# RWKV beta-alpha products made beside the operands, key norms at the key strips, and a 128-row rotary low product

## The chip, the cores and the metric

The kernel is one launch on one core of a Trainium2 chip. The metric is the device time of one execution in microseconds, the median of three runs. Everything is float32; large products are split into a high and a low part (fp32r), so that one product is three matmuls: high by high, low by high, high by low.

## The reference, cut to what matters

Two stacks of layers run one after the other: two hybrid layers, and then four layers of three kinds (SGU, RWKV-7, MLA, SGU) on 512 tokens and 256 context tokens, width 1024. The change touches the RWKV layer and the attention of the MLA layer.

```python
def rwkv7_features(h, mu, w_in, w_lora1, w_lora2, w0, a_lora1, a_lora2, a0, k_k, k_a):
    xx = center_shift(h)
    xs = h[:, :, None, :] + xx[:, :, None, :] * mu
    rkvz = jnp.einsum('blcd,cde->blce', xs[:, :, :4], w_in)
    ...
    decay = jnp.exp(-jnp.exp(log_w.astype(jnp.float32)))
    a = jax.nn.sigmoid(a0[:, None, None, :] + ...)
    kk = split_heads(k * k_k).astype(jnp.float32)
    kk = (kk * lax.rsqrt(jnp.sum(kk * kk, axis=-1, keepdims=True) + 1e-12)).reshape(k.shape)
    k_dir = k * (1 + (a - 1) * k_a)

    def step(S, inp):                       # rwkv7_scan, over time, 2 directions, 16 heads
        w_t, k_t, v_t, kk_t, a_t = inp[:5]
        s_kk = jnp.einsum('nbhvk,nbhk->nbhv', S, kk_t)
        S = S * w_t[..., None, :] - s_kk[..., :, None] * (kk_t * a_t)[..., None, :] + v_t[..., :, None] * k_t[..., None, :]
        y_t = jnp.einsum('nbhvk,nbhk->nbhv', S, inp[5]) if emit else None
        return S, y_t
```

In MLA each head's key has 128 plain and 64 rotary features (`k = concat(k_nope, k_rope)`), and the scores are a product over both.

## The kernel before, in words

The 768 tokens (512 and 256 of context, `T`) are cut into `NS` = 12 steps of `CH` = 64. The features are cut into `KD` = 8 blocks of 128, which are two heads each. The state's recurrence over a step of 64 tokens is turned into products of four operands per direction d: alpha (kk, scaled by decays up to the step) and r, kept side by side in `st_ar`, and beta (kk times a) and k, kept in `st_bk`. `operands(f)` makes them for block f and both directions and stores them to DRAM (`rw_ar`, `rw_bk`).

`features` runs the strips in the order k, r, z, v (8 each; a strip is 48 matmuls). Between the strips it takes turns of `lora`, `operands`, `by_tokens` (the values turned to token order, in the v strips) and `first`. The order of TensorE's instructions is that of the code (`in_order`); the turns are handed out by credits (`OPS`, `PACE`). `operands` has the lora products (L1563) with their tanh (L1564), the norm of the keys by `head_scale` (sums L1233, a reciprocal square root of 12 columns on VectorE L187 to L192, and its spreading over the features L1241, L1245), the decays' scan over time (L1586, L1588), three exponentials (L1594, L1596, L1598), the products (L1604 GpSimd, L1605, L1606, L1609 VectorE) in two parts of 512 and 256 columns, and the stores (L1610 to L1615). `st_ar` and `st_bk` have one buffer each.

`scan` runs 9 slots p. In each, `lanes` steps through block p's first six time steps and block p-1's last six, and side work is woven in: `ahead` (loads and products G, GR, TK for coming steps, L1692 to L1739), `output` of block p-2, and for block p+1 and p+2 the matrix that solves each step's inner recurrence. That is in three parts: `pairs` (L1764: beta times alpha of each step, 64 by 64, from operands read back from DRAM, masked and stored as 32 x 32 blocks to `rw_md`), `inverse` (reads `rw_md`, inverts the 32 x 32 triangles by 31 pairs of vector instructions, stores to `rw_mt`) and `merge` (puts the blocks together with two small products, L1822 and L1834). For block 0 all three and for block 1 the first two are done in the v strips by `first`. SyncE issues all these loads and stores in one queue, in order.

In the MLA heads `attend` computes 64 rows of scores, each over 512 and 256 keys, from five matmuls: three for the plain part, one for the rotary high part over 128 rows (`kr`), and one for the rotary low part over the 64 rows of the head (`krl`), L2284. `by_features` makes `kr` and `krl`; weights are split beside it (`weight_pool`, two raw buffers).

## Time and profile before

| what | value |
|---|---|
| median of 3 runs | 4303.05 us (4300.52 to 4309.85) |
| profiled execution | 4307.25 us, its span 4305.5 us |
| TensorE busy | 3947.2 us, 92% |
| VectorE, ScalarE, GpSimd busy | 2538.4, 1557.5, 1333.9 us |
| RWKV operands beside r and z strips | 2160 to 2450 us |
| v strips | 2452 to 2569 us |
| scan, slots 0 to 8 | 2569 to 3120 us |
| MLA heads | about 3310 to 3890 us |

The times of a trace count from the start of the span. PE is TensorE's matmuls, PEld its weight loads, DVE VectorE, ACT ScalarE, POOL GpSimd, SP SyncE, whose rows are DMA issues. A row of a table of stretches gives its bounds, its length, and then what each engine was busy, with the number of instructions; PEclk is the granted TensorE clock as a share of 2.4 GHz. A row of groups gives line, engine, operation, output and input with their tiles, the count, busy time, mean ns of one, and the idle time in front of them with what ended it. In a timeline row an idle time in front stands in brackets.

### The profile page before, as it was taken

The page shows a single profiled execution, that of the slowest core. Times are in us where ns is not written, and L with a number is a line of the kernel's source. Part 1 is how long each engine was busy: PE and PEld are TensorE (multiplying, and loading weights), DVE is VectorE, ACT ScalarE, POOL GpSimd, SP SyncE. Part 2 cuts the span into 40 slices and gives each one's busy share as a digit, 9 for nine tenths or more (in the row PEclk, how much of TensorE's full clock was granted, in tenths as well). Part 3 has the DMA queues.
Part 4 walks back from the last instruction along what each step waited for, and adds up shares of the span by engine and source line. Part 5 has one row for each costly group of instructions (what it writes and reads, how often), then busy time and mean ns, then how long its engine had stood idle before and what let it go on. Part 6 is the DMA issues. An engine that isn't in the chain of part 4 may idle for free.

```text
span 4305.5 us, 66606 instructions
## 1 busy us (share of the span) xinstructions
PE 3947.2 (92%) x25974; PEld 3217.2 (75%) x25974; DVE 2538.4 (59%) x5080; ACT 1557.5 (36%) x2952; POOL 1333.9 (31%) x1365
## 2 busy tenths in 40 slices
PE   8799999889999999998877787888789999998999
PEld 7777777776877788887755676667567788876887
DVE  7726445765554534445689734677654677784544
ACT  4244223334332322222455322343243455553222
POOL 3321111322211211113455545674122344442221
PEclk9899999899999999999988897999889999999999
DMA  3125543112365321122256676765224121221232
GB/s 90 43 76 159 170 136 90 50 60 94 102 197 157 107 64 59 59 63 86 68 170 182 201 199 152 178 163 123 74 57 127 36 60 49 60 75 52 88 93 88
DMA packets 615143, 447.41 MB, mean 104 GB/s; under 512 B 205469, under 2 KB 544173, under 8 KB 614829
## 3 DMA queue, kind: packets, MB, share of 16 engines
q1 hardware_dynamic: 612236, 438.95, 35.0%
q0 software_dynamic: 2592, 4.20, 0.5%
q8 instruction: 205, 3.36, 0.3%
q14 instruction: 110, 0.89, 0.1%
HBM read 371.76 MB, written 67.11 MB: 102 GB/s over the span
## 4 chain that ended last, share of the span: by engine, by line
PE 75%; DVE 12%; DMA 4%; issue 3%; ACT 3%; POOL 2%; SPq 1%; DVEq 0%; ACTq 0%; POOLq 0%
PE acc L160 54%; PE wide L2284 3%; PE wide L160 2%; PE acc L1717 2%; PE aux L1853 2%; PE po L2332 2%; DMA G<-rw_ar 1%; PE aux L920 1%; PE aux L2309 1%; DVE xs L1347 1%; DVE wlo L141 1%; PE aux L1064 1%; DVE st_bk L1606 1%; DMA rw_bk<-st_bk 1%; DMA ar<-rw_ar 1%
## 5 line engine op out<-in xcount | busy, mean ns | idle before, releaser
L138 ACT CAST whi<-wraw 128x1024 fp32r<-128x1024 f32 (+3 forms) x471 | 456.7, 970 | 1186.5 <-PE acc L160 956.8
L141 POOL TENSOR_TENSOR wlo<-wraw,whi 128x1024 fp32r<-128x1024 f32 (+2 forms) x205 | 427.3, 2085 | 1374.8 <-ACT whi L138 1232.2
L160 PE MATMUL acc<-hh,whi 128*128 128x512 f32 (+2 forms) x1776 | 628.9, 379 | 10.3 <-ACT hh L421 5.0
L160 PE MATMUL acc<-hl,whi 128*128 128x512 f32 (+2 forms) x1776 | 625.4, 377 | 2.5 <-DVE hl L422 2.5
L160 PE MATMUL acc<-hh,wlo 128*128 128x512 f32 (+2 forms) x1776 | 624.7, 376 | 1.7 <-DVE wlo L141 1.7
L141 DVE TENSOR_TENSOR wlo<-wraw,whi 128x1024 fp32r<-128x1024 f32 (+3 forms) x266 | 323.3, 1217 | 469.6 <-ACT whi L138 429.4
L160 PEld LDWEIGHTS acc<-hh,whi 128*128 128x128 f32 (+1 forms) x1776 | 317.2, 189 | 86.8 <-ACT whi L138 16.7
L160 PEld LDWEIGHTS acc<-hh,wlo 128*128 128x128 f32 (+1 forms) x1776 | 316.9, 189 | 64.8 <-DVE wlo L141 2.4
L160 PEld LDWEIGHTS acc<-hl,whi 128*128 128x128 f32 (+1 forms) x1776 | 316.7, 189 | 64.2 <-DVE hl L422 4.1
L160 PE MATMUL acc<-whi,hh 128*128 128x256 f32 (+1 forms) x896 | 295.7, 332 | 2.3 <-ACT hh L967 2.3
L160 PE MATMUL acc<-wlo,hh 128*128 128x256 f32 (+1 forms) x896 | 294.8, 329 | 0.0
L160 PE MATMUL acc<-whi,hl 128*128 128x256 f32 (+1 forms) x896 | 289.4, 326 | 0.4 <-DVE hl L968 0.4
L988 DVE SCALAR_TENSOR_TENSOR xT<-acc,mod,xT 128x512 f32<-128x512 f32 x256 | 185.6, 746 | 134.5 <-PE acc L160 133.7
L160 PEld LDWEIGHTS acc<-whi,hh 128*128 128x128 f32 x896 | 176.3, 197 | 20.3 <-ACT hh L967 4.6
L160 PEld LDWEIGHTS acc<-wlo,hh 128*128 128x128 f32 x896 | 176.6, 197 | 14.1 <-issue 0.7
L160 PEld LDWEIGHTS acc<-whi,hl 128*128 128x128 f32 x896 | 174.9, 196 | 14.6 <-DVE hl L968 1.1
L160 PE MATMUL wide<-xsl,whi 128*128 128x512 f32 (+1 forms) x512 | 141.5, 359 | 31.2 <-POOL xsl L1349 26.2
L160 PE MATMUL wide<-xsh,whi 128*128 128x512 f32 (+1 forms) x512 | 145.9, 368 | 20.4 <-ACT xsh L1348 15.8
L160 PE MATMUL wide<-xsh,wlo 128*128 128x512 f32 (+1 forms) x512 | 140.0, 356 | 3.1 <-POOL wlo L141 2.7
L160 PE MATMUL acc<-ffgh,whi 128*128 128x512 f32 x352 | 139.9, 400 | 0.0
L160 PE MATMUL acc<-ffgl,whi 128*128 128x512 f32 x352 | 138.4, 395 | 0.0
L160 PE MATMUL acc<-ffgh,wlo 128*128 128x512 f32 x352 | 138.3, 395 | 0.0
(627 smaller groups left out, 8972.0 us busy)
## 6 DMA issues: line engine op xcount, KB each, us to landing
ada_w<-in_ada_w SPq DMA_DIRECT2D x32, 1536.0 KB
wraw<-in_sgu_w_in SPq DMA_DIRECT2D x96, 512.0 KB
wraw<-in_w_up SPq DMA_DIRECT2D x88, 512.0 KB
wraw<-in_w_in SPq DMA_DIRECT2D x44, 512.0 KB
wraw<-in_w_down SPq DMA_DIRECT2D x32, 512.0 KB
wraw<-in_sgu_w_out SPq DMA_DIRECT2D x32, 512.0 KB
...
```

Source lines behind the costliest of these rows:

```text
L138: nc.scalar.copy(hi, raw)
L141: eng.tensor_tensor(lo, raw, hi.bitcast(F32), ALU.subtract)
L160: mm(out, lhsT=a, rhs=b[:, t0:t1], start=first and n == 0, stop=last and n == 2)
L920: nc.tensor.matmul(ps[32 * t:32 * t + 32, :384], lhsT=self.sc[:, k * 2 + j, :], rhs=raw[:, j, t * 384:t * 384 + 384], start=k + j == 0, st ...
L988: nc.vector.scalar_tensor_tensor(dst[k], ps, m[:, 16 + k, j:j + 1], dst[k], ALU.mult, ALU.add)
L1064: nc.tensor.matmul(ps[:, c * 128 - t0:c * 128 - t0 + 128], lhsT=v[c][:, ft * 128:ft * 128 + 128], rhs=wst[:, f2, :], start=True, stop=True)
L1347: nc.vector.scalar_tensor_tensor(t[:, t0:t0 + n], self.xx[k][:, t0:t0 + n], mu, src[k], ALU.mult, ALU.add)
L1606: nc.vector.scalar_tensor_tensor(o_(bk[:, s0:s1, 0]), i_(ta[d], t0, n), 0.5, i_(b, t0, n), ALU.mult, ALU.mult)
L1717: nc.tensor.matmul(pk[:, (s - s0) * 256:(s - s0) * 256 + 256], lhsT=bk[:, d, s].rearrange("p q x -> p (q x)"), rhs=G[:, :, d, s], start=Tr ...
L1853: mm = lambda o, d, e, a, b, first=False, last=True: nc.tensor.matmul((ps if o else py)[h[e], o * 128 + d * 64:o * 128 + d * 64 + 64], lhs ...
L2284: nc.tensor.matmul(sc[:, k0:k1], lhsT=a, rhs=b[:, k0:k1], start=j == 0, stop=j == 4)
L2332: nc.tensor.matmul(o, lhsT=a[:, b], rhs=x[:, b], start=b + j == 0, stop=b == NT2 - 1 and j == 2)
```

## The change

Five things are done. (1) The sums for the key norms are made at the k strips (`key_squares`, `key_sums`), and one reciprocal square root over all 96 columns follows at the first r strip; `operands` only spreads them. (2) In `operands` the scan over time runs in place; the exponentials go to a padded tile `eb`, of which a view shifted by one step replaces the subtraction and the third exponential; the products run over all 768 columns; the ec copy goes to GpSimd; the reordering of the chunks moves into the stores (eight in place of four for d = 0). (3) `pairs` and its loads are gone. `within` makes the same products from `st_ar` and `st_bk` in SBUF, called one or two turns after the operands of a direction are made, and stores the diagonal blocks to `md[f]` and the one other block that is needed to `mo[f]`; `merge` reads it from there. No mask is applied, since only the lower parts are read. (4) `inverse` of block p+2 is woven over the whole slot, not its second half, and `first` has one inverse and one merge and no pairs. (5) `krl` has 128 rows and two buffers, and the heads' weights one raw buffer.

```diff
+    def within(self, f, d, ar, bk, tmp):
+        net, nc = self.net, self.net.nc
+        M, hf = tmp(), (slice(0, 64), slice(64, 128))
+        for n0, n in ((0, 8), (8, 4)):
+            pg = net.aux()
+            for s in range(n0, n0 + n):
+                c = s if d else (s - 4) % NS
+                for e in range(2):
+                    nc.tensor.matmul(pg[hf[e], (s - n0) * CH:(s - n0) * CH + CH], lhsT=bk[hf[e], c, 0], rhs=ar[hf[e], c, 0], start=True, stop=True)
+            nc.scalar.copy(M[:, n0 * CH:(n0 + n) * CH], pg[:, :n * CH])
+        Mt = M.rearrange("p (s t) -> p s t", t=CH)
+        for e in range(2):
+            for h in range(2):
+                q = 64 * e + 32 * h
+                nc.sync.dma_start(self.blocks(self.md[f], e, h)[:, d * NS:d * NS + NS], Mt[q:q + 32, :, 32 * h:32 * h + 32])
+            nc.sync.dma_start(self.mo[f][e][:, d * NS:d * NS + NS], Mt[64 * e:64 * e + 32, :, 32:64])
...
+    def key_sums(self, f, sq):
+        nc, ps = self.net.nc, self.net.aux()
+        two = self.bones.rearrange("p (e c) -> p e c", c=64)[:, :, 0]
+        for c in range(NS // 2):
+            nc.tensor.matmul(ps[:, 2 * c:2 * c + 2], lhsT=sq[:, c * 128:c * 128 + 128], rhs=two, start=True, stop=True)
+        nc.vector.tensor_scalar(self.ky[:, f * NS:f * NS + NS], ps[:, :NS], 1.0, 1e-12, ALU.mult, ALU.add)
...
+                if (name, f) == ("r", 0):
+                    net.rsqrt(self.kr, self.ky, Renamed(self.ap, {"rsq_i": "vt", "rsq_t": "vb"}), KD * NS)
...
 # operands
-            return ap.tile([128, T], F32, tag="f", name="tmp", bufs=5)
+            return ap.tile([128, T], F32, tag="f", name="tmp", bufs=4)
...
-        sq = tmp()
-        nc.scalar.activation(sq, kt, AF.Square, scale=col(P["kk"], f))
-        yield
+        if f:
+            yield
+            self.pending()
+            yield
...
-            nc.gpsimd.tensor_tensor(ld, b, ld, ALU.subtract)
...
-            nc.vector.tensor_copy(self.ec[:, f, :, d], ar[:, :, 1, CH - 1])
...
-            nc.scalar.activation(ld, ld, AF.Exp)
...
-            for t0, n, s0, s1 in parts:
-                nc.gpsimd.tensor_tensor(o_(bk[:, s0:s1, 1]), i_(kd, t0, n), i_(b, t0, n), ALU.mult)
-                nc.vector.tensor_tensor(o_(ar[:, s0:s1, 1]), o_(ar[:, s0:s1, 1]), i_(rt, t0, n), ALU.mult)
-                nc.vector.scalar_tensor_tensor(o_(bk[:, s0:s1, 0]), i_(ta[d], t0, n), 0.5, i_(b, t0, n), ALU.mult, ALU.mult)
+            nc.gpsimd.tensor_tensor(o_(bk[:, :, 1]), ch(kd), ch(b), ALU.mult)
+            nc.vector.tensor_tensor(o_(ar[:, :, 1]), eb[:, :, 1:CH + 1], ch(rt), ALU.mult)
+            nc.vector.scalar_tensor_tensor(o_(bk[:, :, 0]), ch(ta[d]), 0.5, ch(b), ALU.mult, ALU.mult)
+            yield
+            nc.vector.tensor_tensor(o_(ar[:, :, 0]), eb[:, :, 2 * d:2 * d + CH], ch(kq), ALU.mult)
...
+            for c0, c1, s0 in parts:
+                at = slice(s0, s0 + c1 - c0)
+                nc.sync.dma_start(steps(self.d["ar"][d, rows, :])[:, at], ar[:, c0:c1])
+                nc.sync.dma_start(steps(self.d["bk"][d, r0:r0 + 64, :])[:, at], bk[0:64, c0:c1])
+                for q in range(2):
+                    nc.sync.dma_start(steps(self.d["bk"][d, r0 + 64:r0 + 128, :])[:, at, 1 - q, :], bk[64:128, c0:c1, q, :])
+            self.pending = partial(self.within, f, d, ar, bk, tmp)
...
 # scan
-                    side += [(pairs(p + 2), 16, PW[0], PW[1]), (inverse(p + 2), 33, 0.5, 1.0)]
+                    side.append((inverse(p + 2), 33))
...
 # MLA
-            with net.weight_pool(2, 3, 3), net.psum(na, nb, nw), ...
+            with net.weight_pool(1, 3, 3), net.psum(na, nb, nw), ...
...
-                    ops = ((ah[:, ct], kh), (ah[:, ct], kl), (al[:, ct], kh), (qs[:, v, ct], kr), (qs[r, v, ct], self.krl[r]))
+                    ops = ((ah[:, ct], kh), (ah[:, ct], kl), (al[:, ct], kh), (qs[:, v, ct], kr), (qs[:, v, ct], krl))
...
-            nc.vector.tensor_tensor(lo[r, t0:t1], ps[r, :t1 - t0], hi[r, t0:t1].bitcast(F32), ALU.subtract)
+            nc.vector.tensor_tensor(lo[:, t0:t1], ps[:, :t1 - t0], hi[:, t0:t1].bitcast(F32), ALU.subtract)
```

On TensorE, in the r strips of the kernel before, one block of operands has these instructions (`hw` and `ha` are the lora products, `bones` the norm's sums, `hs_rep` its spreading; L160 are the strips):

```order
L160 MATMUL wide<-xsh,wlo 128x256
L1563 MATMUL aux<-hw,w_17460 128x512 x2
L1563 MATMUL aux<-hw,w_17460 128x256 x2
L1233 MATMUL aux<-bones,tmp 128x2 x6
L1563 MATMUL aux<-ha,a_17461 128x512 x2
L1563 MATMUL aux<-ha,a_17461 128x256 x2
L160 MATMUL wide<-xsh,whi 128x512
...
L1245 MATMUL aux<-ident,hs_rep 128x128 x6
```

None of them reads a product of the block before. In the changed kernel the same place on TensorE reads as follows (L1668 are the 24 matmuls of one direction, from `st_ar` and `st_bk`):

```order
L160 MATMUL wide<-xsh,wlo 128x256
L1668 MATMUL aux<-st_ar,st_bk 64x64 x24
L1592 MATMUL aux<-hw,w_17559 128x512 x2
L1592 MATMUL aux<-hw,w_17559 128x256 x2
L160 MATMUL wide<-xsh,whi 128x512
...
L1592 MATMUL aux<-ha,a_17560 128x512 x2
L1592 MATMUL aux<-ha,a_17560 128x256 x2
L1253 MATMUL aux<-ident,hs_rep 128x128 x6
L160 MATMUL wide<-xsh,whi 128x512
...
L1668 MATMUL aux<-st_ar,st_bk 64x64 x24
```

The first set is the second direction of the block before, and the lora products of the next block stand directly behind it; the last row is the first direction of that block, three quarters of a strip later.

On SyncE, in slot 1 of the scan, the queue of the kernel before has the store of an inverse (`rw_mt`) ahead of the loads of G (`ar` and `bk` are the loads of `pairs`):

```order
L1676 DMA bk_22141<-rw_bk 128x512
L1798 DMA rw_mt<-invT 96x1024
L1677 DMA ar_22142<-rw_ar 128x4x64
L1797 DMA rw_mt<-invA 96x1024
L1702 DMA G_20707<-rw_ar 64x2x512 x2
L1739 DMA SV<-rw_vt 64x4x64 x4
L1739 DMA VU<-rw_vt 64x4x64 x4
L1774 DMA rw_md<-xx_21242 32x24x32 x4
```

This is the inverse of block 2. In the changed kernel the inverse of block 2 is stored in the v strips already, and that of block 3 in slot 0, where SyncE has this:

```order
L1746 DMA G_20318<-rw_ar 64x2x512 x2
L1783 DMA SV<-rw_vt 64x4x64 x4
L1783 DMA VU<-rw_vt 64x4x64 x4
L1811 DMA rw_mt<-invT 96x1024
L1810 DMA rw_mt<-invA 96x1024
L1823 DMA xx_21694<-rw_mo_16222 32x768
L1736 DMA bk_21609<-rw_bk 128x2x512
```

The pairs' loads and the stores of `rw_md` are gone from the scan, and the inverses stand about one block earlier in the queue.

## Rows read from the trace of the kernel before

**Rows 1.** The page's first line.

```profile
span 4305.5 us, 66606 instructions
```

**Rows 2.** Stretches: us, busy us of PE PEld DVE ACT POOL, granted clock, DMA share, GB/s.

```profile
2160.00:2450.00 290.00, 212.96 (x1037) 169.56 (x1038) 264.13 (x320) 149.29 (x223) 169.38 (x104) 0.82 0.62 187
2452.00:2569.00 117.00, 111.30 (x934) 93.39 (x934) 42.79 (x100) 33.74 (x60) 34.50 (x55) 0.94 0.69 190
2569.00:2627.40 58.40, 40.60 (x595) 32.97 (x596) 18.65 (x65) 15.47 (x44) 27.02 (x54) 0.63 0.82 190
2627.40:2690.50 63.10, 46.66 (x877) 38.27 (x876) 30.60 (x112) 20.09 (x69) 38.04 (x73) 0.83 0.57 132
2690.50:2754.70 64.20, 53.42 (x912) 43.84 (x912) 42.77 (x138) 23.81 (x69) 43.32 (x78) 0.97 0.71 163
2881.10:2946.50 65.40, 56.23 (x936) 46.20 (x932) 46.01 (x145) 24.45 (x72) 43.83 (x76) 0.95 0.60 152
2946.50:3009.20 62.70, 54.71 (x838) 44.30 (x835) 43.55 (x141) 24.92 (x72) 23.79 (x40) 0.92 0.50 120
```

**Rows 3.** The same view of a stretch in the heads.

```profile
3450.00:3550.00 100.00, 100.00 (x578) 81.02 (x576) 78.52 (x187) 51.35 (x120) 44.44 (x38) 1.00 0.22 59
```

**Rows 4.** Timeline, TensorE, heads: start us, us, engine, line, op, out<-in.

```profile
3602.76 0.40 PE L2284 MATMUL wide<-kh,ql 128*128 128x512 f32 x1
3603.00 0.40 PE L2284 MATMUL wide<-kr,qs 128*128 128x512 f32 x1
3603.33 0.50 PE L2284 MATMUL wide<-krl,qs 64*128 64x512 f32 x1
3603.76 0.87 PE L2253 MATMUL acc<-ident,kn 128*128 128x128 f32 x6
3604.83 0.28 PE L2284 MATMUL wide<-kr,qs 128*128 128x256 f32 x1
3605.04 0.38 PE L2284 MATMUL wide<-krl,qs 64*128 64x256 f32 x1
3605.35 0.50 PE L160 MATMUL acc<-oh,whi 128*128 128x512 f32 x1
```

**Rows 5.** Groups, TensorE, 2452:2569: count, busy us, mean ns, idle before and releaser.

```profile
L1764 PE MATMUL aux<-x,xx 64*64 64x64 f32 x96 | 4.3, 230 | 2.7 <-DMA x<-rw_ar 2.7
```

**Rows 6.** Waits, TensorE, first slot: total us, times, longest.

```profile
PE acc L1764 <- DMA ar<-rw_ar: 13.2, 6, 5.1
```

**Rows 7.** Timeline, TensorE, second slot.

```profile
2651.31 1.20 PE L1853 MATMUL aux<-SV,G 128*64 128x64 f32 x16 [6.29 <-ACT SV L1882]
2657.47 2.90 PE L1717 MATMUL acc<-G,bk 128*128 128x256 f32 x6 [3.87 <-DMA G<-rw_ar]
```

**Rows 8.** Timeline, SyncE's DMA issues, second slot.

```profile
2649.08 0.34 SPq L1798 DMA_DIRECT2D rw_mt<-invT  x1
2651.41 1.60 SPq L1702 DMA_DIRECT2D G<-rw_ar  x2
```

**Rows 9.** Groups, TensorE, 2160:2450.

```profile
L1233 PE MATMUL aux<-bones,tmp 128*128 128x2 f32 x96 | 19.3, 329 | 35.5 <-ACT tmp L1564 35.5
```

**Rows 10.** Timeline, VectorE, one block of operands.

```profile
2224.30 1.01 DVE L1618 SCALAR_TENSOR_TENSOR kd<-kd,col_rwkv,ld_r 128x768 f32<-128x768 f32 x1
2254.54 1.01 DVE L1618 SCALAR_TENSOR_TENSOR kd<-kd,col_rwkv,ld_r 128x768 f32<-128x768 f32 x1
```

**Rows 11.** Chain of waits, 2224:2256, shares by line.

```profile
by line: DVE st_bk L1606 21.4%; DMA rw_bk<-st_bk 15.8%; DVE st_ar L1609 11.1%; issue 8.4%; DVE rsq_t L190 7.0%; DVE hs_r L192 6.1%; DVE tmp L1586 5.2%; DVE tmp L1588 5.2%; DVE tmp L1581 4.9%; DVE st_ar L1605 4.2%; DVE wlo L141 3.2%; ACT hs_
```

**Rows 12.** Groups, VectorE, 2160:2450.

```profile
L1606 DVE SCALAR_TENSOR_TENSOR st_bk<-tmp 128x512 f32<-128x512 f32 (+1 forms) x32 | 38.5, 1242 | 3.9 <-DMA rw_bk<-st_bk 2.3 <-issue 1.5
L1595 DVE COPY rw_ec<-st_ar 128x12 f32<-128x12 f32 x16 | 10.5, 657 | 9.6 <-ACT st_ar L1594 9.5
L192 DVE SCALAR_TENSOR_TENSOR hs_r<-rsq_t,hs_r 128x12 f32<-128x12 f32 x24 | 10.2, 426 | 0.7
```

**Rows 13.** Groups, GpSimd, 2160:2450.

```profile
L1590 POOL TENSOR_TENSOR tmp<-tmp 128x768 f32<-128x768 f32 x16 | 34.3, 2144 | 59.0 <-DVE tmp L1586 22.1 <-DVE tmp L1588 21.8 <-ACT tmp L1564 9.6
```

More of the change, by code (lines that the diff above doesn't have):

```diff
@@ L1447, in first @@
         acc = self.net.aux
-        self.masks(cut(X[0], 1280, 128).rearrange("p (q t) -> p q t", t=64))
-        for i, _ in enumerate(self.pairs(0, cur[0], work, acc)):
-            for _ in range(RATE[1] if i else RATE[0]):
-                yield
-        later = self.pairs(1, cur[1], work, acc)
-        next(later)
-        for i, _ in enumerate(self.inverse(cur[0], work, self.net.nc.vector)):
-            if i > 8:
-                next(later, None)
+        for _ in self.inverse(0, cur[0], work, self.net.nc.vector):
             yield
         t = self.big(2)
-        place = {"T1": [cut(t, 0, 768)], "invW": [cut(t, 768, 256), cut(t, 1024, 256)], "TT": [self.big(3)]}
+        place = {"invW": [cut(t, 768, 256), cut(t, 1024, 256)], "TT": [self.big(3)]}
         yield from self.merge(0, cur[0], work, acc)
@@ L1468, in first @@
         self.steps_to_come = self.ahead(cur)
-        inv = self.inverse(cur[1], self.work, self.net.nc.gpsimd)
+        inv = self.inverse(1, cur[1], self.work, self.net.nc.gpsimd)
         for _ in range(9):
@@ L1583, in operands @@
             nc.scalar.activation(ld, ld, AF.Copy, scale=0.5 * DEC, bias=0.5 * DEC)
-            b = tmp()
+            b = ld
+            bb = b if d == 0 else flip(b, 1)
+            nc.vector.tensor_tensor_scan(bb, self.reset, bb, 0.0, ALU.mult, ALU.add)
+            yield
+            eb = self.eb
+            nc.scalar.activation(eb[:, :, 1:CH + 1], ch(b), AF.Exp)
+            nc.scalar.activation(b, b, AF.Exp, scale=-1.0)
             if d == 0:
-                nc.vector.tensor_tensor_scan(b, self.reset, ld, 0.0, ALU.mult, ALU.add)
-            else:
-                nc.vector.tensor_tensor_scan(flip(b, 1), self.reset, flip(ld, 1), 0.0, ALU.mult, ALU.add)
+                parts = ((0, NS - 4, 4), (NS - 4, NS, 0))
+                for c0, c1, s0 in parts:
+                    nc.gpsimd.tensor_copy(self.ec[:, f, s0:s0 + c1 - c0, d], eb[:, c0:c1, CH])
+            else:
+                parts = ((0, NS, 0),)
+                nc.gpsimd.tensor_copy(self.ec[:, f, :, d], flip(eb[:, :, 1], 1))
@@ L1589, in operands @@
             yield
[L1590 removed]
+            if d:
+                self.pending()
             ar = ap.tile([128, NS, 2, CH], F32, tag="st_ar", name="st_ar", bufs=1)
[L1592 to L1596 removed]
@@ L1607, in operands @@
-            yield
-            for t0, n, s0, s1 in parts:
-                nc.vector.tensor_tensor(o_(ar[:, s0:s1, 0]), i_(ld, t0, n), i_(kq, t0, n), ALU.mult)
-            nc.sync.dma_start(self.d["ar"][d, rows, :], ar.rearrange("p s q t -> p (s q t)"))
-            r0 = f * 128
-            nc.sync.dma_start(self.d["bk"][d, r0:r0 + 64, :], bk[0:64].rearrange("p s q t -> p (s q t)"))
-            dst = self.d["bk"][d, r0 + 64:r0 + 128, :].rearrange("p (s q t) -> p s q t", q=2, t=CH)
-            for q in range(2):
-                nc.sync.dma_start(dst[:, :, 1 - q, :], bk[64:128, :, q, :])
+            bk = ap.tile([128, NS, 2, CH], F32, tag="st_bk", name="st_bk", bufs=1)
@@ new lines, in operands @@
+            for c0, c1, s0 in parts:
+                at = slice(s0, s0 + c1 - c0)
[4 more added lines that the diff above has]
+            self.pending = partial(self.within, f, d, ar, bk, tmp)
@@ L1629, in scan @@
             cur = self.cur
-            pairs = lambda k: self.pairs(k, cur[k], self.work, net.acc)
-            inverse = lambda k: self.inverse(cur[k], self.work, nc.gpsimd)
+            inverse = lambda k: self.inverse(k, cur[k], self.work, nc.gpsimd)
             ahead = self.steps_to_come
@@ L1744, in blocks, with inverse @@
         return t[p0:p0 + 24].rearrange("x j i -> j x i")
[L1746 to L1777 removed]
+    def inverse(self, k, cur, work, eng):
         nc = self.net.nc
```

131 lines of the change are left out of this document (55 added, 76 removed).

## The prediction, made before the changed kernel ran

> **What bounds the kernel now.** I went through the page first, then the table of stretches, then, stage by stage, the groups of lines and the timeline. The span is 4305.5 us [rows 1]; the profiled execution took 4307.25 us and the median of the three runs is 4303.05, so the sum below is made against 4307.25 and 4.2 is taken off at the end. The order of the instructions is the same before the key strips and behind the heads, so only about 2050 to 3890 us can change. In the table of stretches [rows 2] the reader is to compare TensorE's busy time with the length of each stretch: in the operand stretch it is 213 of 290 us while VectorE is 264 of 290, so VectorE bounds that stage; in the value strips it is 111 of 117, TensorE bounds; in the first scan slot it is 40.6 of 58.4, in the second 46.7 of 63.1, and from the third on it is 53.4 of 64.2, so the first two have much waiting in them and the later ones some 10 us each. In the heads TensorE is 100 of 100 us at the full granted clock, 2.4 GHz [rows 3]: there every nanosecond that a matmul gives up is span.
>
> **MLA heads, rotary low product over 128 rows: -33 us.** The timeline shows one row of scores [rows 4]. A 128-row matmul over 512 columns starts 0.24 us after the one ahead (3602.76 to 3603.00). The 64-row one starts 0.33 after the matmul ahead, and the next, 128-row again, 0.43 behind it: 0.76 for two that should take 0.47, an excess of 0.29. Over 256 columns it is 0.21 and 0.31, 0.52 against 0.24, an excess of 0.28. There are 64 score rows with one of each: 64 x (0.29 + 0.28) = 36.5 us. Before the change the high product of the same operands already runs over 128 rows; now the low one does too, and VectorE's subtraction that makes it keeps its width per row, so it pays nothing more. With one raw weight buffer in place of two a weight's load can no longer run beside the split of the one before. TensorE is full there and the split weights keep two or three ready, so I take 3 us for it (0 to 12). Net 33, bounds 24 to 38.
>
> **Scan: -46 us.** The pair products leave it: two loads for each of six groups, 48 matmuls and three mask products on VectorE per k. The same work in the value strips has 96 records at 4.3 us for one of two like groups [rows 5], two records to a matmul: 8.6 us for two k and 4.3 for one, and 2.7 of wait on a load. In slot 0 TensorE also stood 13.2 us for its loads [rows 6]: 13.2 + 4.3, less 1.5 that something else will wait for, is -16. In slot 1 the stop between 2642 and 2657 us [rows 7] has two waits, 6.29 and 3.87 us. SyncE's queue shows why [rows 8]: the store of the inverse (rw_mt, 2649.08) stands ahead of the loads of G (2651.41) and waited for GpSimd's inverse, which may start only in the slot's second half. The inverse now reads its input from products made a stage earlier, and in the new order it stands a whole stage earlier; the stores no longer come late. I count -10 (the two waits), with the 4.3 inside it since the slot goes on to wait for other things. Slots 2 to 5 give 4.3 of matmuls and 0.7 (estimate) of the 10.8 us that TensorE idles in such a slot, 4 x 5 = -20. Together -46. Bounds: -66 if each slot gives up its idle time in the first two (18 + 16) and 8 in each later one; -20 if they come down only to slot 6, which has no pairs and no inverse even now and still took 62.7 us against 64.2 and 65.4 [rows 2]. I stay near the middle since slot 6 ran at a lower clock (0.92 against 0.97).
>
> **Value strips: -11 us.** Two sets of pairs, 2 x 4.3 of matmuls, and the 2.7 of wait go from a stretch where TensorE is the bound. Bounds -5 to -18, since the inverse and merge at its end stay and have no cover if the pairs are gone.
>
> **Key strips: +10 us.** Key norms' matmuls move here, from a place where they cost nothing. They cost 19.3 / 8 = 2.4 us of recorded busy time per strip in the operand stretch [rows 9], but records overlap, and between strips without a wait I take 1.25 each: 8 x 1.25 = 10. Bounds 5 to 19.
>
> **Operand stretch: -8 us.** This is the uncertain term. One block of 128 features takes 30.3 us (2224.30 to 2254.54 [rows 10]). The chain through this block shares its 32 us among VectorE's bk products 21%, the wait for the bk stores 16%, ar products 11%, and the square root on 12 columns (L190, L192) 13% [rows 11]. Removed from VectorE in the stretch: the square roots (L192 alone 10.2 us), the ec copy, 10.5 with a wait of 9.6, and the second part of each product: L1606 takes 38.5 us for 32, or 2.4 for two parts [rows 12], while L1618 does a product on all 768 columns in 1.0 [rows 10]. GpSimd loses the subtraction, 34.3 us [rows 13]. With the square roots' 4.2, the copy's 2.5 and three products shorter by up to 1.4 each in two directions, VectorE alone would allow blocks of about 30.3 - 15 = 15 to 20 us.
>
> What takes its place is a loop in series. TensorE now gets 24 matmuls 64 x 64 per direction straight from the st_ar and st_bk buffers, which exist once; they are queued between strips, wait for VectorE's and GpSimd's last product, and behind the second set in the queue stand the next block's lora products, whose tanh starts that block. Before, these did not wait for the products and TensorE ran ahead. What is queued behind a waiting set is the next strip, and the weights' split and z's output behind that. Per block, from the 30.3: -4.2 for the square roots (13% of 32), -4 for the joined products (estimate, half of the gap above), +5.2 for two sets (4.3 x 48/96 = 2.15 of matmuls and some 0.45 of release each), +2 for four more store issues of 0.5 on SyncE (an issue takes 0.34 to 0.8 in [rows 8]). That is 29.3, 8 blocks give -8. Bounds: -45 if the loop hides and TensorE is the bound (213 - 19 of norms + 8 x 4.3 = 228 us of work, some 245 with its prep); +38 at blocks of 35 us, if the loop's links add without overlap. At nothing I count what ScalarE, GpSimd and the DMA engines get: two copies out of PSUM per set, the ec copy, and the md and mo stores, which the slots lose in turn. ScalarE is busy 149 and GpSimd 169 of 290, and the DMA engines 62% [rows 2]; without that room it is rival (b). A matmul over 64 rows between two over 128 costs 0.29 us beyond its columns [rows 4], and the 16 sets stand so between strips; I count nothing for it, since TensorE's queue waits there for the products anyway. The Trainium skill ("TensorEngine Tiling (Array Packing)", Key Properties) has it that a change of the tiling mode drains TensorE, which speaks against sets strewn between strips; at 0.29 each, as an estimate, this stage would come out at -8 + 16 x 0.29 = -3 us by that rule.
>
> **Sum.** -33 - 46 - 11 + 10 - 8 = -88: 4307.25 - 88 = 4219 for a profiled execution, 4215 on the scale of the median.
>
> **Rivals.** (a) The operand loop hides wholly and the stage falls to TensorE's work: -45 in place of -8, 4178. For: VectorE, 264 of 290, loses over 70. Against: TensorE there waits now for ACT's output, 35.5 us in front of the norms [rows 9], so latency, not work, already shows. (b) The loop is bound by latency at 34 us a block: 8 x 4.7 = 38 more, 4253. For: single st_ar and st_bk buffers whose stores already hold up VectorE 16% of the chain; one tmp buffer fewer. (c) The scan gives only -20: 26 more, 4241. For: slot 6. (d) The other side: the new sets block TensorE's queue, the md and mo stores that wait for them block SyncE's queue, and the next strip's weights come behind these. If the next strip then waits each time for six issues and a load, 6 x 0.5 = 3 and some 4 as the wait for G in [rows 7], twice a block, the period goes to 29.3 + 14 = 43 and the stage costs 8 x 14 = 112 more: 4327. It decides from 88 / 8 = 11 us a block. Against: weights have two buffers, and SyncE has room (the new order has some 33 issues a block, at 0.5 each 17 of 30 us).
>
> **How the numbers follow.** Forecast 0.5, (a) 0.15, (b) 0.18, (c) 0.11, (d) 0.06. The forecast's own range, bounds combined, is 4180 to 4245; with (a) and most of (b) in it, 4160 to 4262. Within 0.2% (8.6 us, what a measurement of this kernel tells from no change) lies the edge between (b) and (d), 0.03; slower only (d), 0.05; faster 0.92.
>
> **What would show it.** MLA: the krl matmul starts 0.23 after kr and the next 0.23 behind it, and the heads are 30 to 36 us shorter. Scan: no pair matmuls, the waits of slots 0 and 1 gone, their lengths near 42 and 53 us. Operands: L1618's successor at a distance of 26 to 33 us, and TensorE's longest waits in front of the 64 x 64 sets, released by VectorE or GpSimd. Key strips: norm matmuls between them and a stretch longer by 5 to 19. The prediction is wrong if the blocks go above 35 us, if slots stay above 62, or if the heads wait for raw weights.

## The result, and the profile after

The changed kernel takes 4250.64 us (median of 4 runs, 4246.21 to 4251.30) against 4302.46 for the kernel before: ratio 0.9869, 95% interval 0.9853 to 0.9885, so 52 us faster, where 88 were forecast. The profiled span went from 4305.5 to 4244.2 us, 61.3 less. Stage by stage, in the two profiles (starts of the first instruction of each stage on TensorE):

| stretch | before | after | change | forecast |
|---|---|---|---|---|
| to the first key strip | 2044.8 | 2039.5 | -5.3 | 0 |
| key strips (eight) | 103.9 | 112.5 | +8.6 | +10 |
| to the first lora product | 16.7 | 15.2 | -1.5 | 0 |
| operands, to the first value strip | 267.9 | 265.3 | -2.6 | -8 |
| value strips, to the first scan step | 135.7 | 135.7 | 0 | -11 |
| scan slots 0 and 1 | 120.4 | 92.5 | -27.9 | -26 |
| scan slots 2 to 5 | 257.2 | 256.2 | -1.0 | -20 |
| scan slots 6 to 8 | 151.9 | 149.1 | -2.8 | 0 |
| to the first score | 232.6 | 235.6 | +3.0 | 0 |
| heads | 567.8 | 535.0 | -32.8 | -33 |
| rest | 406.7 | 407.7 | +1.0 | 0 |

The first line is ahead of all instructions that the change touches. The changed kernel's own repeat (below) starts its strips at 2040.5, and a later kernel with the same code there (four buffers, below) at 2045.5, so I credit none of it to the change; what moves it is open.

The table of stretches of the changed kernel, for the operands, the value strips and slots 0 to 5 (columns as in [rows 2]):

```profile
2167.00:2432.00 265.00, 203.99 (x1651) 162.69 (x1650) 186.54 (x157) 137.74 (x207) 138.84 (x86) 0.93 0.77 206
2432.00:2568.00 136.00, 116.28 (x788) 95.70 (x786) 64.41 (x110) 43.54 (x69) 94.36 (x154) 0.92 0.68 185
2568.20:2612.60 44.40, 35.70 (x498) 27.94 (x500) 16.79 (x60) 14.89 (x43) 33.62 (x59) 0.65 0.61 150
2612.60:2660.70 48.10, 40.28 (x764) 33.09 (x762) 26.91 (x105) 18.42 (x67) 36.31 (x70) 0.89 0.46 104
2660.70:2726.50 65.80, 57.01 (x835) 46.19 (x834) 42.87 (x138) 23.71 (x71) 41.21 (x71) 0.89 0.53 122
2726.50:2793.30 66.80, 58.09 (x836) 46.73 (x834) 43.27 (x141) 24.60 (x72) 41.15 (x71) 0.87 0.49 121
2793.30:2853.30 60.00, 51.06 (x840) 41.08 (x836) 42.99 (x142) 24.62 (x72) 43.30 (x76) 1.00 0.54 135
2853.30:2916.90 63.60, 54.94 (x838) 44.26 (x834) 42.56 (x143) 24.58 (x72) 12.10 (x20) 0.92 0.49 122
```

VectorE has fallen from 264 of 290 us [rows 2] to 187 of 265: it no longer bounds the operands. The value strips are as long as before (135.7 us) although TensorE has less to do, 115.8 us busy where it had 121.6, and GpSimd has 94 us of work there where it had 50 over the same stretch. The 117 us of [rows 2] begin 19 us after the first value strip. Slots 0 and 1 are 44 and 48 us long. Slots 2 and 3 ran at a granted clock of 0.89 and 0.87 where slot 2 before had 0.97 [rows 2]. Slots 3 and 4 of the kernel before, for comparison:

```profile
2754.70:2818.70 64.00, 55.23 (x932) 45.12 (x928) 44.60 (x144) 24.33 (x72) 44.08 (x76) 0.97 0.69 167
2818.70:2881.10 62.40, 53.91 (x934) 43.93 (x930) 44.87 (x144) 24.07 (x72) 42.00 (x74) 1.00 0.72 171
```

One row of scores in the changed kernel's heads, which answers to [rows 4] (timeline of TensorE):

```profile
3557.83 0.40 PE L2296 MATMUL wide<-kh,ql 128*128 128x512 f32 x1
3558.06 0.39 PE L2296 MATMUL wide<-kr,qs 128*128 128x512 f32 x1
3558.29 0.39 PE L2296 MATMUL wide<-krl,qs 128*128 128x512 f32 x1
3558.52 0.82 PE L2266 MATMUL acc<-ident,kn 128*128 128x128 f32 x6
3559.54 0.29 PE L2296 MATMUL wide<-kr,qs 128*128 128x256 f32 x1
3559.66 0.28 PE L2296 MATMUL wide<-krl,qs 128*128 128x256 f32 x1
3559.78 0.39 PE L160 MATMUL acc<-oh,whi 128*128 128x512 f32 x1
```

The low product starts 0.23 us after the high one over 512 columns and 0.12 over 256, and the next matmul follows after 0.23 and 0.12: the excess is gone, as forecast.

VectorE's last product of two successive blocks of operands (answers to [rows 10]):

```profile
2220.82 1.00 DVE L1654 SCALAR_TENSOR_TENSOR kd<-kd,col_rwkv,ld_r 128x768 f32<-128x768 f32 x1
2251.10 1.01 DVE L1654 SCALAR_TENSOR_TENSOR kd<-kd,col_rwkv,ld_r 128x768 f32<-128x768 f32 x1
```

Two successive blocks lie 30.3 us apart. The others are 29.6, 28.4, 28.8, 29.9 and 30.9, without the one in which the z strips begin (46.7, before 44.8): 29.3 was forecast. Before, the blocks beside the r strips lay 30.1 to 30.3 apart, as in [rows 10], but those beside the z strips 34.3, 32.3 and 26.8. TensorE's waits in front of the new sets, in the r strips (2152 to 2293) and the z strips (2293 to 2433), total us, times, longest:

```profile
PE aux L1668 <- DVE st_bk L1636: 18.2, 6, 4.9
...
PE aux L1668 <- DVE st_bk L1636: 21.7, 7, 4.6
```

These 40 us stand where the kernel before waited 35.5 in front of the norms [rows 9].

At the end of the value strips, SyncE's issues in the changed kernel:

```profile
2554.21 0.34 SPq L1811 DMA_DIRECT2D rw_mt<-invT  x1
2556.34 0.33 SPq L1810 DMA_DIRECT2D rw_mt<-invA  x1
...
2560.03 0.38 SPq L1531 DMA_DIRECT2D ld_s<-rw_ks  x1
```

And what TensorE waits for there:

```profile
2564.77 2.90 PE L1553 MATMUL aux<-ld_s,bones 128*128 128x512 f32 x4 [4.51 <-DMA ld_s<-rw_ks]
```

The two stores of block 2's inverse wait for GpSimd at the head of SyncE's queue; the load of ld_s is issued behind them and TensorE stands 4.5 us for it. It is the pattern of [rows 7, 8], one stage earlier. A second wait is new in the value strips, in front of the turning of the values to token order (L1542; before, that had none):

```profile
PE aux L1542 <- DVE rst L1554: 3.7, 2, 2.2
PE aux L1542 <- ACT vt L1545: 3.3, 2, 2.9
```

TensorE's waits for loads in slots 2 to 5, before:

```profile
PE acc L1717 <- DMA G<-rw_ar: 9.8, 6, 3.0
PE acc L1764 <- DMA ar<-rw_ar: 9.3, 6, 4.0
```

And after:

```profile
PE acc L1761 <- DMA G<-rw_ar: 16.4, 11, 3.0
PE acc L1761 <- DMA SV<-rw_vt: 3.9, 1, 3.9
```

19.1 us of waiting have become 20.3: the loads of the pairs are gone, and those of G and SV take their place. One such wait, and the granted clock ahead of it, behind it and later:

```profile
2733.20 2.34 PE L1761 MATMUL acc<-G,bk 128*128 128x256 f32 x6 [3.05 <-DMA G<-rw_ar]
```

```profile
2720.00:2730.20 10.20, 9.79 (x164) 7.49 (x160) 6.32 (x18) 5.90 (x14) 7.09 (x15) 1.00 0.73 141
2733.80:2744.00 10.20, 10.20 (x72) 8.56 (x71) 5.77 (x25) 1.74 (x8) 0.00 (x0) 0.50 0.80 239
2744.00:2750.00 6.00, 5.26 (x100) 4.36 (x101) 3.68 (x14) 3.87 (x9) 3.82 (x10) 1.00 0.33 100
```

After 3.05 us without work the clock is at 1.2 GHz (0.50) for 10.2 us, in which TensorE is busy throughout: some 5 us of full-speed work (an estimate, half of the 10.2) are lost on top of the 3. Not every such wait has this price: one of 3.0 us at 2797 lies in slot 4, which ran at 1.00.

### The profile page after: what moved, and what is told of

Its sections match the earlier page's. It is cut to its first block, busy times and chain, and to the rows that moved or that the text cites. A ratio compares the mean times of both kernels' runs of the same rounds, so it can differ in the third digit from the quotient of the medians.

```text
span 4244.2 us, 66522 instructions
## 1 busy us (share of the span) xinstructions
PE 3896.4 (92%) x25974; PEld 3206.0 (76%) x25974; DVE 2468.1 (58%) x4915; ACT 1558.8 (37%) x2952; POOL 1322.4 (31%) x1354
## 5 line engine op out<-in xcount | busy, mean ns | idle before, releaser
L160 PE MATMUL acc<-hh,whi 128*128 128x512 f32 (+2 forms) x1776 | 628.5, 379 | 9.9 <-ACT hh L421 5.0
L160 PE MATMUL acc<-hl,whi 128*128 128x512 f32 (+2 forms) x1776 | 624.6, 376 | 2.1 <-DVE hl L422 2.1
L160 PE MATMUL acc<-hh,wlo 128*128 128x512 f32 (+2 forms) x1776 | 624.1, 376 | 1.6 <-DVE wlo L141 1.6
L160 PEld LDWEIGHTS acc<-hh,whi 128*128 128x128 f32 (+1 forms) x1776 | 316.9, 189 | 86.3 <-ACT whi L138 16.9
L160 PEld LDWEIGHTS acc<-hh,wlo 128*128 128x128 f32 (+1 forms) x1776 | 316.5, 188 | 64.7 <-DVE wlo L141 2.4
L160 PEld LDWEIGHTS acc<-hl,whi 128*128 128x128 f32 (+1 forms) x1776 | 316.7, 189 | 63.5 <-DVE hl L422 3.8
L160 PE MATMUL acc<-whi,hh 128*128 128x256 f32 (+1 forms) x896 | 296.1, 333 | 2.3 <-ACT hh L967 2.3
L160 PE MATMUL acc<-wlo,hh 128*128 128x256 f32 (+1 forms) x896 | 295.3, 330 | 0.0
L160 PE MATMUL acc<-whi,hl 128*128 128x256 f32 (+1 forms) x896 | 290.4, 328 | 0.4 <-DVE hl L968 0.4
L160 PEld LDWEIGHTS acc<-whi,hh 128*128 128x128 f32 x896 | 176.6, 198 | 20.3 <-ACT hh L967 4.6
L160 PEld LDWEIGHTS acc<-wlo,hh 128*128 128x128 f32 x896 | 176.9, 197 | 14.1 <-issue 0.7
L160 PEld LDWEIGHTS acc<-whi,hl 128*128 128x128 f32 x896 | 175.6, 196 | 14.9 <-DVE hl L968 1.1
L160 PE MATMUL wide<-xsh,whi 128*128 128x512 f32 (+1 forms) x512 | 146.9, 370 | 16.8 <-ACT xsh L1373 16.8
L160 PE MATMUL wide<-xsl,whi 128*128 128x512 f32 (+1 forms) x512 | 140.6, 357 | 14.8 <-POOL xsl L1374 10.1
L1761 PE MATMUL acc<-G,bk 128*128 128x256 f32 x368 | 118.7, 457 | 33.1 <-DMA G<-rw_ar 19.2
L160 PE MATMUL acc<-ffgh,whi 128*128 128x512 f32 x352 | 139.9, 400 | 0.0
L160 PE MATMUL wide<-xsh,wlo 128*128 128x512 f32 (+1 forms) x512 | 138.5, 353 | 0.0
L160 PE MATMUL acc<-ffgl,whi 128*128 128x512 f32 x352 | 138.4, 395 | 0.0
```

Of the source, the lines that this page charges most:

```text
L160: mm(out, lhsT=a, rhs=b[:, t0:t1], start=first and n == 0, stop=last and n == 2)
L1761: nc.tensor.matmul(pk[:, (s - s0) * 256:(s - s0) * 256 + 256], lhsT=bk[:, d, s].rearrange("p q x -> p (q x)"), rhs=G[:, :, d, s], start=Tr ...
```

## The experiments

**The MLA part alone**, on the kernel before: the lines of part (5) of the change.

```diff
-                    ops = (..., (qs[:, v, ct], kr), (qs[r, v, ct], self.krl[r]))
+                    ops = (..., (qs[:, v, ct], kr), (qs[:, v, ct], krl))
...
```

> The kernel before with the MLA part of the change alone (128-row rotary low product, two krl buffers, one raw weight buffer). If the 64-row matmul's excess of 0.57 us per score row is the whole of it: heads shorter by 31 to 35 us, everything ahead of 3300 us as before, ratio 0.992 to 0.993. If part of the heads' 33 us in the changed kernel came from the RWKV part (another clock, another phase of the loads): under 25 us, ratio above 0.994.

Ratio 0.9941 (0.9926 to 0.9956), -25 us by the median: the interval holds the ratios of both theories and does not part them. The heads took 537.1 us, 30.7 less:

```profile
3341.50:3878.60 537.10, 507.73 (x3189) 446.06 (x3189) 425.46 (x1061) 280.00 (x703) 234.13 (x194) 0.99 0.22 60
```

TensorE, which was busy 553.8 of 567.8 us there, now is 507.7 of 537.1. By the heads' own length it is the first theory, just short of its 31 us and well over the 25 of the second. The span fell by 20.0 only: the other 10.7 us are longer stretches of unchanged code, 6 of them in the scan, 4 between it and the first score.

**Pair matmuls put back** into the changed kernel's slots 0 to 5, from a constant.

```diff
+    def dummies(self):
...
+        for i in range(6):
+            if i % 2 == 0:
+                pg = self.net.acc()
+            for s in range(4):
+                for e in range(2):
+                    c = 256 * (i % 2) + 64 * s
+                    self.net.nc.tensor.matmul(pg[hf[e], c:c + 64], lhsT=self.bones[hf[e], 0:64], rhs=self.bones[hf[e], 64:128], start=True, stop=True)
...
+                    side.append((self.dummies(), 12, 0.0, 0.45))
```

> The changed kernel, with 48 matmuls 64 x 64 put back into each of the slots 0 to 5, from a constant in SBUF: no loads, no mask, no store, results unused. If the pair matmuls were worth the 5 us a slot that the prediction took: +30 us over the six slots. If their price at equal clock is what slot 4 shows (62.4 before, 60.0 after): +2.4 a slot, +15. If only the loads and waits of the pairs cost: 0 to +4, and slots 0 and 1 stay at 44 and 48 us.

Ratio 0.9936 (0.9921 to 0.9951). Slots 0 to 5 together take 369.1 us against 348.7 and 345.3 in two profiles of the changed kernel: 3.4 to 4.0 a slot, between the first and the second theory. By length alone this is not clear of noise, since kernels with the very scan code of the changed kernel took 345 to 377 us for these slots (see "The changed kernel again"). Clearer is TensorE's busy time counted at full speed, each piece of it times the clock granted in it (an estimate, worked out from the traces): 278.2 us in slots 0 to 5 before, 260.7 and 261.2 in the two profiles of the changed kernel, 280.5 with the matmuls back. That is 2.8 to 3.3 us a slot, near the second theory. Slots 0, 2 and 3:

```profile
2574.00:2622.60 48.60, 36.88 (x594) 29.83 (x596) 16.51 (x59) 14.92 (x41) 36.05 (x67) 0.71 0.61 143
2673.20:2742.80 69.60, 58.27 (x934) 47.23 (x931) 43.24 (x139) 24.25 (x72) 42.84 (x79) 0.93 0.50 119
2742.80:2811.90 69.10, 60.05 (x936) 48.35 (x933) 44.31 (x141) 24.69 (x73) 42.63 (x76) 0.90 0.50 118
```

Even with all 48 matmuls back slot 0 stays at 48.6 us, against 58.4 [rows 2]: the larger part of that slot's 14 us were the loads and what waited for them. A share is not to be had, since the slot took 44.0 to 51.3 us in kernels with the same scan code and no such matmuls. TensorE's waits for G in slots 2 to 5 did not shrink either (20.5 us), so the pairs' matmuls by themselves do not hide G's loads.

**Norms back in the block**: `head_scale` in `operands`, none at the key strips.

```diff
+        sq = self.ap.tile([128, S + C], F32, tag="vt", name="ksq", bufs=1)
+        nc.scalar.activation(sq, kt, AF.Square, scale=col(P["kk"], f))
...
+        hs = self.head_scale(ap, sq, 1.0, 1e-12, net.aux, net.aux, "kq")
```

> The changed kernel, with the key norms' sums and the reciprocal square roots of 12 columns back in each block of operands, and none at the key strips. If the square roots lie on the block's chain (4.2 us in the prediction): blocks of 33 to 34 us instead of 29.5, key strips 8.6 us shorter, +20 to +27 us. If VectorE does them while it waits for the lora tanh (32 us of idle time in front of the scans over time): blocks unchanged, key strips 8.6 us shorter, -6 to -9 us.

Ratio 0.9917 (0.9900 to 0.9934), slower than the two measurements of the changed kernel by 14 to 21 us in the ratio and by 22 to 26 in the median. Key strips 104.1 us (8.4 shorter), operands 295.4 (30 longer), blocks of 32.4, 33.2, 34.2, 38.7, 33.3 and 33.4. VectorE's waits:

```profile
DVE kq L1591 <- PE aux L1253: 30.8, 8, 5.9
DVE hs_y L1238 <- PE aux L1235: 29.9, 8, 5.8
```

The norm is on the chain: VectorE waits 30 us for the sums and 31 for the spread norms, where the changed kernel has 1.4 us of wait for the spread norms and no sums. Half of that takes the place of the 32 us that it waited there in front of the scans over time (2.0 here), as the second theory has it; the other half is longer blocks. The first theory holds. The run does not part the square root from the sums and the spreading.

**Lora products first**: the next block's lora products ahead of the second set in TensorE's queue.

```diff
-        if f:
-            yield
-            self.pending()
-            yield
...
+        if f:
+            self.pending()
+            yield
         hs = finish(hs)
...
-        M, hf = tmp(), (slice(0, 64), slice(64, 128))
+        M, hf = self.ap.tile([128, S + C], F32, tag=("vt", "ld_s")[d], name="wm", bufs=1), (slice(0, 64), slice(64, 128))
```

> The changed kernel, with the next block's lora products ahead of the second set of 64 x 64 products in TensorE's queue, and the sets' copies in two buffers of their own, not in the ring of the tanh results. If the loop in series (set, lora, tanh, scan, products) bounds the operand stage: blocks of 24 to 26 us instead of 29.5, waits in front of the sets under 20 us instead of 40, -25 to -35 us. If the queue of SyncE (182 of 265 us issuing) or the stores' landing bounds it: blocks 28 us or more, 0 to -10 us.

Neither: ratio 0.9959 (0.9946 to 0.9972), 32 to 44 us slower than the changed kernel (32 between the profiles), 6 to 9 of it up to the first scan step and the rest in the scan. The waits in front of the sets fell to 19 us, as the first theory has it, but the blocks did not follow: two are shorter (26.7 and 25.2), the others 32 to 46, with the place where the z strips begin. VectorE waits, in the operand stretch:

```profile
DVE tmp L1612 <- ACT tmp L1608: 21.8, 7, 4.7
DVE kq L1597 <- DMA ld_k<-rw_k: 12.5, 3, 6.5
```

and ScalarE:

```profile
ACT eb L1616 <- DVE st_ar L1636: 27.3, 5, 9.8
```

The loop's other links take over: the one `eb` buffer, and loads that come late. So the order of the lora products is not what holds the block alone. Why the scan, whose code is the same, took 523 us is not settled; slots 2 to 5 had 69 us each.

**The changed kernel again**, as a yardstick.

> The changed kernel once more, unaltered, beside the three below on the same chip: the yardstick for differences of a few us. Every theory: ratio within 0.985 to 0.989, stages within 4 us of the first profile except where the granted clock differs between slots of the scan.

Ratio 0.9885 (0.9864 to 0.9905). Up to the first scan step 3.1 us later, scan 491.3 against 497.7. Slot 3 took 61.9 us at a clock of 0.94 where it had 66.8 at 0.87, and slot 4 64.4 at 0.92 where it had 60.0 at 1.00, each with the same idle time of TensorE, 8.7 to 8.9 us. So one profile's slot is uncertain by 4 to 5 us, by the clock alone.

The scan as a whole is less certain still. Four of the other kernels have the changed kernel's scan code word for word, and it took 508.4 (the md and mo stores by ScalarE), 509.3 (norms in the block), 512.2 (sets twice) and 523.3 us (lora first) in them. TensorE's busy time at full speed is the same in all six profiles, 377 to 379 us (an estimate, as above); what differs is waiting and the clock. Why is open. A scan between 491 and 523 us in one profile by itself tells nothing about an edit.

**Merge's loads by ScalarE.**

```diff
+            eng = nc.scalar if k else nc.sync
-            nc.sync.dma_start(M[64 * e:64 * e + 32], self.mo[k][e])
+            eng.dma_start(M[64 * e:64 * e + 32], self.mo[k][e])
...
```

> The changed kernel with merge's loads (blocks of the inverse and of md and mo) issued by ScalarE for blocks 1 to 7, not by SyncE. If slots 2 to 5 lost what the pairs gave back because these loads (about 8 us of issuing) stand ahead of G's in SyncE's queue, and the idle time drops the clock to 1.2 GHz: waits for G under 1 us, granted clock 0.95 or more in slots 2 to 5, these slots 60 to 61 us each, scan 8 to 15 us shorter. If G waits for its buffer or the transfer itself: the waits of 3 us stay, scan within 4 us.

Ratio 0.9912 (0.9895 to 0.9929). The waits for G stay (slots 2 to 5, total, times, longest):

```profile
PE acc L1761 <- DMA G<-rw_ar: 19.5, 11, 5.2
```

and the scan is 520 us long, more than the second theory's 4 us away but inside the spread above. So merge's loads, which stood ahead of G's in SyncE's queue, are not what makes G late; the scan's length decides nothing.

**The inverse's stores by GpSimd.**

```diff
-        nc.sync.dma_start(mt[0], A)
-        nc.sync.dma_start(mt[1], Tm)
+        nc.gpsimd.dma_start(mt[0], A)
+        nc.gpsimd.dma_start(mt[1], Tm)
```

> The changed kernel with the stores of the inverse (rw_mt) issued by GpSimd, which computes it, not by SyncE. If the value strips lost the 11 us of the pairs because SyncE's queue stands behind these stores (ld_s issued at 2560.03, 4.5 us of wait for it): that wait gone, first scan step 4 to 7 us earlier against the strips. If GpSimd's issuing costs more than that (it computes the inverse at the same time): no gain, the inverses 2 to 4 us longer each.

Ratio 0.9920 (0.9904 to 0.9936). From the first value strip to the first scan step 129.0 us, against 135.7 and 133.8: the wait for ld_s is gone, the first theory holds for the value strips. The inverses of blocks 1 and 2 took GpSimd no longer (54 and 40 us from first to last instruction, 54 and 41 in the changed kernel), so the second theory's price does not show. The scan took 528.8 us, 5 more than the spread above reaches: that these stores cost something there is possible and not shown.

**The md and mo stores by ScalarE.**

```diff
-                nc.sync.dma_start(self.blocks(self.md[f], e, h)[...
+                nc.scalar.dma_start(self.blocks(self.md[f], e, h)[...
-            nc.sync.dma_start(self.mo[f][e][...
+            nc.scalar.dma_start(self.mo[f][e][...
```

> The changed kernel with the stores of the new products (md, mo, 96 of them) issued by ScalarE, not by SyncE. If SyncE's queue bounds the operand stage (182 of 265 us issuing, 57 of these for md and mo): blocks of 25 to 27 us instead of 29.5, 15 to 30 us off. If the series of set, lora, tanh, scan and products bounds it, ScalarE's 57 us of issuing lie on it: blocks of 30 to 34 us, 0 to 30 us more.

Ratio 0.9996 (0.9984 to 1.0009): the whole gain is gone. The operands took 313.5 us, 48 more, in blocks of 39.2, 33.7, 37.4, 36.8, 34.9 and 38.9 us: the way of the second theory, but for the most part beyond its 34 us a block, and beyond its 30 us in all. ScalarE in one of them:

```profile
2232.67 0.97 ACTq L1674 DMA_DIRECT2D rw_md<-tmp  x2
2233.68 1.56 ACTq L1675 DMA_DIRECT2D rw_mo<-tmp  x1
2235.28 2.25 ACTq L1674 DMA_DIRECT2D rw_md<-tmp  x2
2237.57 1.28 ACTq L1675 DMA_DIRECT2D rw_mo<-tmp  x1
2238.89 0.80 ACT L1513 COPY rst<-wide 128x768 f32<-128x768 f32 x1 [6.25 <-DMA rw_md<-tmp]
```

Six issues take 6 us, in which the engine does nothing else: they are the 6.25 us of idle time in front of the copy behind them. So ScalarE's time is on the chain; all 96 issues took it 67 us, where SyncE needed 57. SyncE, with these 57 us less to issue, gave nothing back that shows. That its queue does not bound the stage is not shown by this alone, since what it lost ScalarE got at once.

**Four buffers for G, SV and VU** in the scan.

```diff
-        fresh = self.groups < 4
+        fresh = self.groups < 5
...
-        G, GR, TK = self.gs[(self.groups - 1) % 3], tile("GR", 2, 4, 2, CH), tile("TK", 2, 2, 4, CH)
-        VU, SV = tile("VU", 2, 2, 4, CH), tile("SV", 2, 2, 4, CH)
+        G, GR, TK = self.gs[(self.groups - 1) % 4], tile("GR", 2, 4, 2, CH), tile("TK", 2, 2, 4, CH)
+        VU, SV = tile("VU", 2, 2, 4, CH, bufs=4), tile("SV", 2, 2, 4, CH, bufs=4)
```

> The changed kernel with four buffers in place of three for the scan's loaded operands (G, SV, VU). If slots 2 to 5 kept their length because TensorE now stands earlier at the products and waits for G and SV, whose loads wait for the buffer of three groups before (waits 20 to 22 us over these slots), and because each such wait lowers the clock: waits under 6 us, granted clock 0.97 or more, slots 57 to 60 us, scan 15 to 30 us shorter, 4220 to 4240 us. If the loads wait for SyncE's queue or the steps' own chain sets the slot: waits move to other lines, scan within 5 us.

4233.39 us, ratio 0.9822 (0.9802 to 0.9842), clear of the changed kernel's interval. The scan is 477.0 us, below the whole spread above; the next kernel, which has the four buffers too, repeats it (477.2). Slots 1, 2, 3 and 5, and TensorE's three largest waits in slots 2 to 5:

```profile
2625.30:2666.60 41.30, 38.30 (x764) 31.51 (x762) 27.07 (x105) 17.87 (x66) 31.25 (x57) 0.95 0.50 122
2666.60:2733.00 66.40, 56.74 (x840) 45.26 (x836) 42.72 (x140) 24.38 (x72) 48.01 (x87) 0.87 0.52 127
2733.00:2793.40 60.40, 53.21 (x836) 42.50 (x832) 41.56 (x141) 24.58 (x72) 40.72 (x70) 0.94 0.59 134
2855.50:2914.00 58.50, 53.40 (x838) 43.00 (x836) 41.33 (x143) 24.79 (x72) 10.39 (x16) 0.94 0.57 133
```

```profile
PE acc L1235 <- ACT ysq L1930: 6.6, 2, 5.4
PE aux L1867 <- DVE VU L1880: 6.0, 8, 0.8
PE acc L160 <- ACT yh L177: 5.3, 2, 2.7
```

G and SV are no longer waited for at all, and the scan is 14 to 21 us shorter: so far the first theory. Its other signs did not come: the clock is 0.87 to 0.95 in slots 2 to 5 and not 0.97, and slots 2 to 4 take 60 to 66 us and not 57 to 60. TensorE's idle time in slots 2 to 5 fell only from 35.1 and 38.1 us to 30.6, though 20 us of waits are gone: others grew in their place, the output's chain (ysq, yh) foremost. Slot 2 stayed long, at a clock of 0.87 and with GpSimd at 48 us; that is not settled. Whether four buffers fit the kernel before, and what they would give there, was not run.

**The same, with the stores of the inverses 1 and 2 by GpSimd** (those that fall in the value strips).

```diff
-        nc.sync.dma_start(mt[0], A)
-        nc.sync.dma_start(mt[1], Tm)
+        out = nc.gpsimd if k in (1, 2) else nc.sync
+        out.dma_start(mt[0], A)
+        out.dma_start(mt[1], Tm)
```

> The same with the inverse's stores of blocks 1 and 2, which fall in the value strips, issued by GpSimd. If the wait for ld_s at the end of the value strips is SyncE standing behind these stores: first scan step 4 to 6 us earlier than in the kernel with four buffers alone. Otherwise within 1.5 us of it.

Ratio 0.9825 (0.9806 to 0.9845), 4231.26 us. From the first value strip to the first scan step 130.0 us against 133.7: 3.7 shorter, just short of the first theory's 4 to 6 and well over the second's 1.5; in the whole time it is lost in the noise.

**Every set made twice.**

```diff
-            for s in range(n0, n0 + n):
+            for s in [*range(n0, n0 + n), *range(n0, n0 + n)]:
```

> The changed kernel with every set of 64 x 64 products in the operand stage made twice into the same place. If the sets stand in the series loop with their full price (2.15 us each in the prediction): 16 x 2.15 = +34 us, blocks 33 to 34 us. If TensorE's part of the loop is hidden behind VectorE and the stores: 0 to +8 us, blocks under 31 us, and the wait in front of the strips shrinks instead.

Ratio 0.9999 (0.9986 to 1.0012), some 50 us slower than the changed kernel (49 to 56 by ratio and median); 42 to 45 of it lie ahead of the first scan step, 35 of them in the operands and 5 to 7 in the value strips, which have no sets. Blocks of 31.9, 36.1, 34.1, 34.9, 33.9 and 37.8. TensorE's waits in the operand stretch:

```profile
PE aux L1253 <- ACT tmp L1593: 38.2, 13, 5.1
PE aux L1668 <- DVE st_bk L1636: 17.6, 9, 4.3
```

The sets cost their full price in the operands, 35 / 16 = 2.2 us each against 2.15 taken: nothing hides them.

## Why the prediction was right, and where it was too large

52 us came of 88. The measured median of 4250.64 us lies above the forecast's own bounds, 4180 to 4245, and inside the wider range, 4160 to 4262, only because that takes in most of rival (b). By its time (b), 4253, is the nearest of all; by its mechanism, blocks of 34 us, it did not come. The heads, the key strips and slots 0 and 1 were forecast rightly, by their mechanism too; that the whole time still lies in the wider range is owed to a rival that did not happen, and so in part to luck.

- **Heads, -33:** right, -32.8 and, alone, -30.7. Both sides of the 64-row matmul lost their excess. The single raw buffer cost little that shows: no wait for a raw weight appears, and for split ones 1.3 us (one more of 4.5 in the part alone). What shows instead is VectorE's part of the plain keys, which TensorE now reaches early: 10.3 us of wait in front of their transposes, where there was none.
- **Operands, -8:** the mechanism and the block were right (29.3 forecast, 28.4 to 30.9 measured), the term was not: -2.6. The blocks gained 9 us from the first lora product to the last product; 6.5 came back behind them, since TensorE used to run ahead and now has a set and one and a half strips behind the last block, where it had one strip. The prediction has no term for this end. That the loop's links stand in series is shown by the sets made twice, the norms put back and the md and mo stores; that it is not the order of the lora products alone, by the run with these first. The Trainium skill ("TensorEngine Tiling (Array Packing)", Key Properties) states that a change of the tiling mode drains TensorE. By the prediction's estimate of 0.29 us a set the term would have been -3 by that rule, near the -2.6; but no run here tells a drain at the sets from the waits around them, and the give-back is seen elsewhere.
- **Key strips, +10:** right, +8.6.
- **Slots 0 and 1, -26:** right, -27.9, though as 14 and 14 us and not 16 and 10. The inverse's stores come a stage earlier and the loads of the pairs are gone. Kernels with the same scan code took 92.5 to 101.4 us here, against 120.4 and 123.7 in two profiles with the scan of before: the gain is sure, its size within 9 us.
- **Slots 2 to 5, -20:** this is the step that failed: "Slots 2 to 5 give 4.3 of matmuls and 0.7 (estimate) of the 10.8 us that TensorE idles in such a slot". Taking the pairs away shortened the slots by 0.3 us each (1.2 in the second profile). The table splits the 257 us into what they are made of, worked out from the traces (estimates): TensorE's idle time, its busy time counted at full speed, and the rest, which is what the time at 1.2 GHz cost.

| slots 2 to 5 | length | idle | busy at full speed | cost of the clock |
|---|---|---|---|---|
| before | 257.1 | 37.2 | 213.3 | 6.6 |
| the MLA part alone (scan of before) | 258.2 | 35.7 | 212.7 | 9.8 |
| changed | 256.2 | 35.1 | 201.4 | 19.7 |
| changed, again | 252.3 | 38.1 | 202.0 | 12.2 |
| changed, pair matmuls back | 269.9 | 37.1 | 214.7 | 18.1 |
| changed, four buffers | 247.4 | 30.6 | 201.9 | 14.9 |
| the same, stores of inverses 1 and 2 by GpSimd | 244.6 | 35.3 | 203.9 | 5.4 |

  The matmuls were worth 2.8 to 3.0 us a slot and not 4.3, the idle time gave up nothing, and the lower clock took back 2 to 13 us, by the profiles that are compared, for which the prediction has no term. Slots 2, 3 and 5 stayed above 62 us, which it had named as a sign of being wrong. The idle time stays because TensorE arrives earlier at the products and waits for G and SV, whose loads cannot start before the buffer of three groups earlier is free: with four buffers these waits vanish. That brings these slots 10 to 13 us below the kernel before, half of the 20 or a little more, so the buffers are a part of the cause and not the whole. Why the clock is lower in the changed scan, though its idle time is the same, is not shown; that it often falls in or behind a wait is. Rival (c), a scan that gives 20, spoke of this stage; the scan's 32 us lie between it and the forecast.
- **Value strips, -11:** failed too, 0 measured, outside its bounds. The prediction held that TensorE bounds this stretch, and that its matmuls are therefore the price. It read that from 117 us that begin 19 us late; over the whole stretch TensorE was busy 121.6 of 135.7 us. It became 5.8 us less busy, and all of that went into waits. The inverses of blocks 1 and 2 moved there, and with them the stop that they make in SyncE's queue, named in the prediction for slot 1 and not looked for in the order of the value strips, where it could be read: 4.5 us for ld_s. With these stores on GpSimd's queue 4 to 7 us come back. Another 7.0 us are the new waits for VectorE and ScalarE in front of the turning of the values; no run takes them away, so their cause stays open.

Rivals (a), (b) and (d) did not come in the operands: neither did the loop hide, nor was it longer than its links.
